# GpSimd makes the low part of a weight tile in four operations of 256 columns in place of one of 1024

## The chip, the cores and the metric

The kernel runs on one core of a Trainium2 chip. The metric is the device time of one launch in microseconds (us). Of the kernel before, three timed runs gave 2517.66, 2519.01 and 2524.25 us, so the median is 2519.01 us.

## The reference, cut to what matters

One layer of a decoder trunk on 256 tokens of width 2048, all in float32. The part that the change touches is the second sub-layer, a retrieval of experts by product keys (cut):

```python
def peer(h, w_q, sub_keys, w_up, w_down):
    qp = (h @ w_q).reshape(B, S, PEER_HEADS, 2, PEER_HALF)
    s = jnp.einsum('bshpe,hpne->bshpn', qp, sub_keys)
    v1, i1 = lax.top_k(s[..., 0, :], PEER_TOPK)
    v2, i2 = lax.top_k(s[..., 1, :], PEER_TOPK)
    cand = (v1[..., :, None] + v2[..., None, :]).reshape(B, S, PEER_HEADS, -1)
    top, ci = lax.top_k(cand, PEER_TOPK)
    idx = e1 * PEER_NKEYS + e2              # e1, e2: the two key numbers of ci
    g = jax.nn.softmax(top, axis=-1)
    # per token: 128 of 16384 experts, one row of w_up and one of w_down each
    a = gelu(einsum('td,tkd->tk', x, w_up[idx]))
    return einsum('tk,tkd->td', g * a, w_down[idx])
```

The first sub-layer (convolution, dilated attention, gates) comes before it and holds none of the changed operations.

## The kernel before

Every float32 product is made of three products of rounded parts: a weight tile is split into `hi`, the tile rounded, and `lo`, the tile less `hi`, and TensorE multiplies hi by hi, lo by hi and hi by lo. Weights stream from memory in units of 128x2048; a unit has two halves of 128x1024 columns, and a half is the step of the program. For each half ScalarE makes `hi` (`split_a`, L84), then VectorE or GpSimd makes `lo` (`split_b`, L88), then TensorE runs the products (`mm`). The class `Stream` writes the instructions of each engine in a fixed order: `hi` is written three halves and `lo` two halves ahead of the products, and background work of VectorE (`spread`) is put between. There are four buffers of `hi` and three of `lo`.

The retrieval does not gather: it multiplies with all 16384 experts and weighs with a gate matrix that is zero for those not chosen. The up products run over four quarters of 32 units (`up_unit`). There a unit must be transposed first: VectorE writes `wt` (L1250, two buffers), ScalarE and GpSimd read it. A half is 24 matmuls: for each of 8 blocks of 128 columns L1265 (hi), L1266 (hi again, other factor) and L1267, which uses 128 columns of `lo` as its weights.

Which engine makes `lo` is chosen by `pool_lo`. GpSimd makes it for all 64 halves of the first quarter and the first 36 of the second (100 in a row, with nothing else to do on GpSimd but one IOTA), for 16 halves of the last quarter, and for one half of two in the second pass of the down products of three quarters (`down_unit`, 48 halves). VectorE makes the others.

Beside the 100 halves VectorE has two background works: the top-16 search (L1134 to L1224, up to about 1160 us) and then, one step behind each half, the gate matrix (`gate_c`): five tensor_tensor operations, L1331, L1334 and three times L1338, whose results feed 24 small matmuls (L1347), which TensorE runs after that half's products, and L1354, which reads the product from PSUM.

Of the kernel before, what the change touches and what calls it, by code (L numbers as in the profile page):

```python
# [8 lines left out]
F32 = mybir.dt.float32  # L9
# [5 lines left out]
OP = mybir.AluOpType  # L15
# [51 lines left out]
def layer_kernel(ctx, tc, x, c, norm1_g, norm2_g, w_ada, b_ada, w_in, conv_dw, conv_db, conv_ln_g,  # L67
                 conv_ln_b, w_conv_out, b_conv_out, q_norm_g, k_norm_g, w_attn_o, w_out, peer_w_q,
                 peer_sub_keys, peer_w_up, peer_w_down, out):
    nc = tc.nc  # L70
# [14 lines left out]

    def split_b(h, src, eng):
        h.lo = main.tile([P, 1024], F32R, name="lo", tag="lo", bufs=LO_BUFS)
        eng.tensor_tensor(h.lo, src, h.hi.bitcast(F32), op=OP.subtract)  # L88

    turn = [0]  # L90

# [6 lines left out]
    def weight_unit(w_ap, mm, after=((), ()), pool_lo=(False, False)):  # L98

        u = Unit(None, [])  # L100

        def load():
            raw = load_raw()
            view = raw.rearrange("p (a b) -> p a b", a=4)
            if isinstance(w_ap, list):
                for i, ap in enumerate(w_ap):
                    part = view[32 * i:32 * (i + 1)] if ap.ap[0][1] == 32 else view[:, :, P * i:P * (i + 1)]
                    nc.sync.dma_start(part, ap)
            else:
                nc.sync.dma_start(view, w_ap)  # L110
            u.raw = raw

        u.load = load
        for n in range(2):
            h = Half(mm=lambda h, n=n: mm(n, h.hi.rearrange("p (a b) -> p a b", a=2),
                                          h.lo.rearrange("p (a b) -> p a b", a=2)),
                     after=after[n])
            h.a = lambda h, n=n: split_a(h, u.raw[:, n * 1024:(n + 1) * 1024])
            h.b = lambda h, n=n: split_b(h, u.raw[:, n * 1024:(n + 1) * 1024],
                                         nc.gpsimd if pool_lo[n] else nc.vector)  # L120
            h.unit = u
            u.halves.append(h)
        return u
# [421 lines left out]
    def start_half(u, n, blk, k, k0, k1):  # L545

        src = lambda: u.raw[:, n * 1024:(n + 1) * 1024]

        def mm(h):
            hi, lo = (w.rearrange("p (a b) -> p a b", a=2) for w in (h.hi, h.lo))  # L550
            if k == k0:
                blk.open(k0)
            for t in range(2):
                z = blk.ps[t]
                for kk in range(2):
                    first, last = blk.ends(k + kk, k0, k1)
                    nc.tensor.matmul(z, lhsT=h_hi(k + kk, t), rhs=hi[:, kk], start=first, stop=False)
                    nc.tensor.matmul(z, lhsT=h_hi(k + kk, t), rhs=lo[:, kk], start=False, stop=False)
                    nc.tensor.matmul(z, lhsT=h_lo(k + kk, t), rhs=hi[:, kk], start=False, stop=last)  # L559

        h = Half(mm=mm, a=lambda h: split_a(h, src()), b=lambda h: split_b(h, src(), nc.vector))
        if k == k1 - 2:
            h.after = [lambda: blk.close(k0, k1)]
        u.halves.append(h)
# [668 lines left out]
    def up_unit(q, r, pool_lo):  # L1233
# [11 lines left out]
        for n in range(2):  # L1245
            h = Half(mm=None, uses_raw_in="a")

            def a(h, n=n):
                wt = T2["pool"].tile([P, 8, 4, 32], F32, name="wt", tag="wt", bufs=2)
                nc.vector.transpose(wt.rearrange("p j g a -> p g j a"),  # L1250
                                    u.raw.rearrange("p (g j a) -> p g j a", g=4, a=32)[:, :, n * 8:(n + 1) * 8, :])
                cell[n] = wt.rearrange("p j g a -> p (j g a)")
                split_a(h, cell[n])

            def b(h, n=n):
                split_b(h, cell[n], nc.gpsimd if pool_lo(r, n) else nc.vector)

            def mm(h, n=n):
                if n == 0 and r % 2 == 0:
                    C["ps"] = T2["ps"].tile([P, 2, T], F32, name="aps", tag="qp", bufs=2)  # L1260
                z = C["ps"][:, r % 2, :]
                hi, lo = (v.rearrange("p (j e) -> p j e", j=8) for v in (h.hi, h.lo))
                for jj in range(8):
                    j = 8 * n + jj
                    nc.tensor.matmul(z, lhsT=hi[:, jj], rhs=qh["hi"][:, j, :], start=j == 0, stop=False)  # L1265
                    nc.tensor.matmul(z, lhsT=hi[:, jj], rhs=qh["lo"][:, j, :], start=False, stop=False)  # L1266
                    nc.tensor.matmul(z, lhsT=lo[:, jj], rhs=qh["hi"][:, j, :], start=False, stop=j == NK - 1)  # L1267

            h.a, h.b, h.mm = a, b, mm
            if n == 1 and r % 2 == 1:  # L1270
                h.after = [lambda: up_done(q, r - 1, C["ps"])]
            u.halves.append(h)
# [343 lines left out]
```

## Time and profile before

| what | value |
|---|---|
| median of three runs | 2519.01 us |
| profiled execution | 2518.21 us, its span 2516.4 us |
| TensorE busy | 2426.6 us (96%) |
| VectorE busy | 1854.2 us (74%) |
| ScalarE busy | 1120.8 us (45%) |
| GpSimd busy | 530.3 us (21%) |
| tensor_tensor of L88 on GpSimd | 116 with `wt` (mean 2529 ns), 48 with `raw` (mean 2436 ns) |
| granted TensorE clock | 0.989 of full speed, mean |

PE is TensorE's matmuls, PEld its weight loads, DVE VectorE, ACT ScalarE, POOL GpSimd. A matmul's row shows a modelled end, so a busy PE can hide short gaps: its pace is better read from the starts. In a timeline, rows are merged where one engine repeats a line; the bracket gives idle time before the row and what ended it.

### The profile page before, as it was taken

The page shows a single profiled execution, that of the slowest core. Times are in us where ns is not written, and L with a number is a line of the kernel's source. Part 1 is how long each engine was busy: PE and PEld are TensorE (multiplying, and loading weights), DVE is VectorE, ACT ScalarE, POOL GpSimd, SP SyncE. Part 2 cuts the span into 40 slices and gives each one's busy share as a digit, 9 for nine tenths or more (in the row PEclk, how much of TensorE's full clock was granted, in tenths as well). Part 3 has the DMA queues.
Part 4 walks back from the last instruction along what each step waited for, and adds up shares of the span by engine and source line. Part 5 has one row for each costly group of instructions (what it writes and reads, how often), then busy time and mean ns, then how long its engine had stood idle before and what let it go on. Part 6 is the DMA issues. An engine that isn't in the chain of part 4 may idle for free.

```text
span 2516.4 us, 39750 instructions
## 1 busy us (share of the span) xinstructions
PE 2426.6 (96%) x15728; PEld 2056.6 (82%) x15728; DVE 1854.2 (74%) x2642; ACT 1120.8 (45%) x1477; POOL 530.3 (21%) x262
## 2 busy tenths in 40 slices
PE   7999889999999899988999999999999999999998
PEld 4667677777766799988889988999987899988877
DVE  2655679886454569897998787877799777667776
ACT  5333345444334444443335555555443344445454
POOL 1000000000000007786552234332000111124023
PEclk9999999999999999999999999999999999999999
DMA  9887346777899978777557866899844777766563
GB/s 329 297 301 251 117 136 210 257 251 267 279 298 294 204 159 178 158 167 152 110 124 220 234 218 194 222 226 238 204 156 135 185 181 185 188 186 214 194 209 117
DMA packets 261178, 518.73 MB, mean 206 GB/s; under 512 B 16400, under 2 KB 57568, under 8 KB 260352
## 3 DMA queue, kind: packets, MB, share of 16 engines
q1 hardware_dynamic: 258912, 507.61, 70.4%
q0 software_dynamic: 2048, 8.58, 1.0%
q8 instruction: 123, 2.02, 0.4%
q14 instruction: 63, 0.52, 0.1%
q10 hardware_dynamic: 32, 0.01, 0.0%
HBM read 511.94 MB, written 4.19 MB: 205 GB/s over the span
## 4 chain that ended last, share of the span: by engine, by line
PE 71%; DVE 10%; POOL 3%; issue 2%; DMA 1%; ACT 1%; SPq 0%; DVEq 0%; POOLq 0%; ACTq 0%
PE aps L1267 6%; PE aps L1265 6%; PE aps L1266 6%; PE y L1435 6%; PE y L1436 6%; PE y L1438 5%; PE z L429 5%; PE z L431 4%; PE z L430 4%; PE z L1436 3%; PE z L1438 3%; PE z L1435 3%; POOL lo L88 3%; DVE wt L1250 2%; PE ada L330 2%
## 5 line engine op out<-in xcount | busy, mean ns | idle before, releaser
L88 DVE TENSOR_TENSOR lo<-raw,hi 128x1024 fp32r<-128x1024 f32 x456 | 561.8, 1237 | 376.3 <-issue 112.6
L84 ACT CAST hi<-raw 128x1024 fp32r<-128x1024 f32 x504 | 526.6, 1051 | 520.6 <-PE zv L559 103.1
L1267 PE MATMUL aps<-h2hi,lo 128*128 128x256 f32 x2048 | 582.0, 284 | 8.6 <-POOL lo L88 8.5
L1265 PE MATMUL aps<-h2hi,hi 128*128 128x256 f32 x2048 | 584.3, 285 | 0.4 <-ACT hi L84 0.4
L1266 PE MATMUL aps<-h2lo,hi 128*128 128x256 f32 x2048 | 580.7, 284 | 0.0
L84 ACT CAST hi<-wt 128x1024 fp32r<-128x1024 f32 x256 | 269.3, 1052 | 470.7 <-DVE wt L1250 427.6
L88 POOL TENSOR_TENSOR lo<-wt,hi 128x1024 fp32r<-128x1024 f32 x116 | 292.7, 2529 | 611.1 <-PE aps L1267 497.1
L1267 PEld LDWEIGHTS aps<-h2hi,lo 128*128 128x128 f32 x2048 | 394.0, 192 | 11.2 <-POOL lo L88 11.2
L1265 PEld LDWEIGHTS aps<-h2hi,hi 128*128 128x128 f32 x2048 | 394.1, 192 | 2.6 <-ACT hi L84 0.6
L1266 PEld LDWEIGHTS aps<-h2lo,hi 128*128 128x128 f32 x2048 | 394.3, 193 | 2.0 <-issue 0.2
L1250 DVE STREAM_TRANSPOSE wt<-raw 128x1024 f32<-128x1024 f32 x256 | 315.8, 1237 | 28.2 <-POOL lo L88 23.7
L1418 DVE TENSOR_TENSOR ccl<-C,cch 128x256 fp32r<-128x256 f32 x248 | 198.9, 803 | 96.7 <-PE z L1438 57.6
L1435 PE MATMUL y<-hi,cch 128*128 128x512 f32 x608 | 241.1, 397 | 0.0
L1436 PE MATMUL y<-lo,cch 128*128 128x512 f32 x608 | 237.3, 390 | 0.0
L88 DVE TENSOR_TENSOR lo<-wt,hi 128x1024 fp32r<-128x1024 f32 x140 | 171.8, 1229 | 27.3 <-PE aps L1267 14.0
L1438 PE MATMUL y<-hi,ccl 128*128 128x512 f32 x608 | 187.6, 390 | 0.0
L88 POOL TENSOR_TENSOR lo<-raw,hi 128x1024 fp32r<-128x1024 f32 x48 | 117.0, 2436 | 245.9 <-PE z L1436 123.6
L347 POOL TENSOR_TENSOR acc<-acc,raw 128x512 f32<-128x512 f32 x60 | 101.4, 1689 | 261.0 <-ACT raw L346 240.3
L1413 ACT CAST cch<-C 128x256 fp32r<-128x256 f32 x248 | 99.8, 403 | 123.6 <-PE z L1436 101.9
L1436 PE MATMUL z<-lo,cch 128*128 128x512 f32 x384 | 149.5, 389 | 2.2 <-DVE lo L88 2.2
L1435 PE MATMUL z<-hi,cch 128*128 128x512 f32 x384 | 149.5, 389 | 1.0 <-ACT cch L1413 1.0
L1438 PEld LDWEIGHTS y<-hi,ccl 128*128 128x128 f32 x608 | 114.2, 188 | 24.4
(295 smaller groups left out, 3965.7 us busy)
## 6 DMA issues: line engine op xcount, KB each, us to landing
raw<-in_peer_w_up_dram SPq DMA_DIRECT2D x512, 256.0 KB, 6.0
raw<-in_peer_w_down_dram SPq DMA_DIRECT2D x128, 1024.0 KB, 5.1
raw<-in_w_ada_dram SPq DMA_DIRECT2D x86, 1024.0 KB, 7.1
raw<-in_w_in_dram SPq DMA_DIRECT2D x73, 1024.0 KB, 5.3
raw<-in_w_out_dram SPq DMA_DIRECT2D x64, 256.0 KB, 5.2
raw<-in_peer_w_q_dram SPq DMA_DIRECT2D x64, 256.0 KB, 7.1
raw<-in_w_in_dram SPq DMA_DIRECT2D x22, 512.0 KB, 8.9
raw<-in_w_ada_dram SPq DMA_DIRECT2D x20, 512.0 KB, 5.2
```

Source lines behind the costliest of these rows:

```text
L84: nc.scalar.copy(h.hi, src)
L88: eng.tensor_tensor(h.lo, src, h.hi.bitcast(F32), op=OP.subtract)
L347: nc.gpsimd.tensor_tensor(acc, acc, src, op=OP.add)
L429: nc.tensor.matmul(z, lhsT=ah, rhs=hi[:, kk], start=first, stop=False)
L1250: nc.vector.transpose(wt.rearrange("p j g a -> p g j a"), u.raw.rearrange("p (g j a) -> p g j a", g=4, a=32)[:, :, n * 8:(n + 1) * 8, :])
L1265: nc.tensor.matmul(z, lhsT=hi[:, jj], rhs=qh["hi"][:, j, :], start=j == 0, stop=False)
L1266: nc.tensor.matmul(z, lhsT=hi[:, jj], rhs=qh["lo"][:, j, :], start=False, stop=False)
L1267: nc.tensor.matmul(z, lhsT=lo[:, jj], rhs=qh["hi"][:, j, :], start=False, stop=j == NK - 1)
L1418: nc.vector.tensor_tensor(cl, row, ch, op=OP.subtract)
L1435: nc.tensor.matmul(z, lhsT=ch, rhs=hi, start=first, stop=False)
L1436: nc.tensor.matmul(z, lhsT=ch, rhs=lo, start=False, stop=False)
L1438: nc.tensor.matmul(z, lhsT=cl, rhs=hi, start=False, stop=last)
```

## The change

`split_b` issues, where the engine is GpSimd, four subtractions of 256 columns on slices of the same three tiles. On VectorE it stays at one of 1024.

```diff
     def split_b(h, src, eng):
         h.lo = main.tile([P, 1024], F32R, name="lo", tag="lo", bufs=LO_BUFS)
-        eng.tensor_tensor(h.lo, src, h.hi.bitcast(F32), op=OP.subtract)
+
+        n = 256 if eng is nc.gpsimd else 1024
+        for i in range(0, 1024, n):
+            eng.tensor_tensor(h.lo[:, i:i + n], src[:, i:i + n], h.hi[:, i:i + n].bitcast(F32), op=OP.subtract)
```

On GpSimd, at the start of the up products, `lo<-wt,hi` stands for the operation of L88 and the bracket names the engines on whose counts it waits. Before:

```order
L1068 IOTA iota_rep 128x256
L88 TENSOR_TENSOR lo<-wt,hi 128x1024 [waits PE_49,Activation_49] x9
L1161 IOTA small_7763 128x256
L88 TENSOR_TENSOR lo<-wt,hi 128x1024 [waits PE_49,Activation_49] x91
L347 TENSOR_TENSOR acc<-acc,raw 128x512 [waits DMAHW5_49,Activation_49]
```

The same place with the change, where the line is L91 and the rows around the second IOTA are shown:

```order
L91 TENSOR_TENSOR lo<-wt,hi 128x256 [waits PE_49,Activation_49]
L91 TENSOR_TENSOR lo<-wt,hi 128x256 x3
L1164 IOTA small_7790 128x256
L91 TENSOR_TENSOR lo<-wt,hi 128x256 [waits PE_49,Activation_49]
L91 TENSOR_TENSOR lo<-wt,hi 128x256 x3
```

The first piece of a half waits for what the whole operation waited for, and the other three wait for nothing; the order of the halves is the same.

On TensorE, at the start of a half in the same stretch, before:

```order
L1265 MATMUL aps<-h2hi,hi 128x256 [waits Activation_49]
L1266 MATMUL aps<-h2lo,hi 128x256
L1267 MATMUL aps<-h2hi,lo 128x256 [waits Pool_49]
L1265 MATMUL aps<-h2hi,hi 128x256
L1266 MATMUL aps<-h2lo,hi 128x256
```

With the change, at the end of a half and the start of the next one (L1268 to L1270 are the same three lines):

```order
L1268 MATMUL aps<-h2hi,hi 128x256
L1269 MATMUL aps<-h2lo,hi 128x256
L1270 MATMUL aps<-h2hi,lo 128x256 [waits Pool_49]
L1268 MATMUL aps<-h2hi,hi 128x256
L1269 MATMUL aps<-h2lo,hi 128x256
L1270 MATMUL aps<-h2hi,lo 128x256
L1268 MATMUL aps<-h2hi,hi 128x256
L1269 MATMUL aps<-h2lo,hi 128x256
L1270 MATMUL aps<-h2hi,lo 128x256
L1268 MATMUL aps<-h2hi,hi 128x256 [waits Activation_49]
L1269 MATMUL aps<-h2lo,hi 128x256
L1270 MATMUL aps<-h2hi,lo 128x256 [waits Pool_49]
```

A half waited once for GpSimd, at its first matmul with `lo`; now it waits four times, at each sixth matmul, once for each piece. No instruction of VectorE, ScalarE, TensorE or of the DMA queues changes its place.

## Rows read from the trace of the kernel before

**Rows 1.** The page: span, busy time by engine, and the larger group of L88.

```profile
span 2516.4 us, 39750 instructions
PE 2426.6 (96%) x15728; PEld 2056.6 (82%) x15728; DVE 1854.2 (74%) x2642; ACT 1120.8 (45%) x1477; POOL 530.3 (21%) x262
...
L88 POOL TENSOR_TENSOR lo<-wt,hi 128x1024 fp32r<-128x1024 f32 x116 | 292.7, 2529 | 611.1 <-PE aps L1267 497.1
```

**Rows 2.** Windows: length, busy PE, PEld, DVE, ACT, POOL, clock, DMA share.

```profile
952.00:1160.00 208.00, 199.01 (x1629) 195.82 (x1628) 180.12 (x342) 87.70 (x99) 168.96 (x68) 1.00 0.80 171
...
1212.00:1316.00 104.00, 97.92 (x1154) 92.57 (x1153) 100.01 (x164) 35.20 (x57) 60.54 (x24) 1.00 0.53 122
...
1480.00:1610.00 130.00, 129.00 (x669) 110.73 (x668) 98.68 (x90) 70.33 (x99) 52.82 (x23) 1.00 0.67 198
```

**Rows 3.** Waits of TensorE, 952 to 1160 us: total, times, longest.

```profile
PE aps L1267 <- POOL lo L88: 8.5, 11, 1.9
```

**Rows 4.** Waits of TensorE, 1160 to 1316 us.

```profile
PE gps L1347 <- DVE ohg L1338: 11.9, 7, 4.2
```

**Rows 5.** Timeline of GpSimd in the up products: start, duration of the row, operation.

```profile
952.17 2.41 POOL L88 TENSOR_TENSOR lo<-wt,hi 128x1024 fp32r<-128x1024 f32 x1 [81.24 <-PE qp L1100]
...
1069.91 2.36 POOL L88 TENSOR_TENSOR lo<-wt,hi 128x1024 fp32r<-128x1024 f32 x1 [5.46 <-ACT hi L84]
...
1149.36 17.33 POOL L88 TENSOR_TENSOR lo<-wt,hi 128x1024 fp32r<-128x1024 f32 x7 [3.06 <-ACT hi L84]
```

**Rows 6.** Timeline of GpSimd: a tensor_tensor of 512 columns after an idle time.

```profile
1334.71 1.29 POOL L347 TENSOR_TENSOR acc<-acc,raw 128x512 f32<-128x512 f32 x1 [23.39 <-ACT raw L346]
```

**Rows 7.** Timeline of GpSimd: two memsets, one behind the other, at the start.

```profile
3.17 0.54 POOL L297 MEMSET silu_c<- 128x512 f32 x1
3.63 0.32 POOL L444 MEMSET uT<- 128x240 f32 x1
```

**Rows 8.** Timeline of VectorE: one operation blocked, the same one shortly after.

```profile
1021.38 3.05 DVE L1206 TENSOR_TENSOR C<-C,small 128x1024 bf16<-128x1024 bf16 x1
...
1029.87 1.23 DVE L1206 TENSOR_TENSOR C<-C,small 128x1024 bf16<-128x1024 bf16 x1
```

**Rows 9.** Timeline of VectorE beside the seven operations of GpSimd from 1149.36.

```profile
1162.79 1.70 DVE L1331 TENSOR_TENSOR oh<-iota_rep,e2T 128x1024 bf16<-128x1024 bf16 x1
1164.41 2.56 DVE L1334 TENSOR_TENSOR oh<-iota_rep,e1T 128x512 bf16<-128x512 bf16 x1
```

**Rows 10.** Timeline of VectorE: a gate step with GpSimd idle.

```profile
1184.37 1.23 DVE L1250 STREAM_TRANSPOSE wt<-raw 128x1024 f32<-128x1024 f32 x1
...
1185.84 0.67 DVE L1331 TENSOR_TENSOR oh<-iota_rep,e2T 128x1024 bf16<-128x1024 bf16 x1
1186.44 0.41 DVE L1334 TENSOR_TENSOR oh<-iota_rep,e1T 128x512 bf16<-128x512 bf16 x1
1186.88 1.09 DVE L1338 TENSOR_TENSOR ohg<-oh,gp 128x512 bf16<-128x512 bf16 x3
1187.89 1.24 DVE L1250 STREAM_TRANSPOSE wt<-raw 128x1024 f32<-128x1024 f32 x1
```

**Rows 11.** Timeline of GpSimd in the gate steps.

```profile
1174.20 2.62 POOL L88 TENSOR_TENSOR lo<-wt,hi 128x1024 fp32r<-128x1024 f32 x1 [7.51 <-PE aps L1267]
...
1214.69 2.40 POOL L88 TENSOR_TENSOR lo<-wt,hi 128x1024 fp32r<-128x1024 f32 x1 [1.28 <-PE aps L1267]
...
1244.50 2.58 POOL L88 TENSOR_TENSOR lo<-wt,hi 128x1024 fp32r<-128x1024 f32 x1 [1.71 <-PE aps L1267]
...
1308.75 2.58 POOL L88 TENSOR_TENSOR lo<-wt,hi 128x1024 fp32r<-128x1024 f32 x1 [1.71 <-PE aps L1267]
```

**Rows 12.** Timeline of VectorE: a gate step with GpSimd at work.

```profile
1240.45 1.24 DVE L1250 STREAM_TRANSPOSE wt<-raw 128x1024 f32<-128x1024 f32 x1
...
1241.92 1.42 DVE L1331 TENSOR_TENSOR oh<-iota_rep,e2T 128x1024 bf16<-128x1024 bf16 x1
...
1244.73 1.24 DVE L1250 STREAM_TRANSPOSE wt<-raw 128x1024 f32<-128x1024 f32 x1
```

## The prediction

> **What bounds the kernel now.** I read the page first, then windows by stage, then what TensorE waited for in each stage, then the timelines of GpSimd and VectorE where it waited. On the page TensorE is busy 96% of the span, VectorE 74%, GpSimd 21% [rows 1], which says that GpSimd matters only locally. The windows show where. From 1480 to 1610 us, the second down pass of the first quarter, TensorE is busy for 129.00 of 130 us [rows 2]: what GpSimd does there costs nothing as long as it is on time. The two stages in which GpSimd makes every low part are different. From 952 to 1160 us TensorE lacks 9.0 us of 208, and 8.5 us of that are 11 waits for GpSimd's `lo` [rows 2, 3]; GpSimd is busy for 168.96 us there. From 1212 to 1316 us VectorE is busy for 100.01 of 104 us and TensorE for 97.92 [rows 2]: the gate steps are bound by VectorE, and between 1160 and 1316 us TensorE waits 11.9 us for its L1338 [rows 4]. So the change is worth what it does in about 364 us, in two stages with different limits.
>
> **The price of four pieces.** The trace has no subtraction of 256 columns. An operation that starts after an idle time takes 2.41 us for 1024 columns [rows 5] and 1.29 us for 512 [rows 6]: 1.12 us for 512 columns more, so 0.17 us are fixed, and a piece is 0.17 + 0.56 = 0.73 us. Four after each other would be 2.92 us. But durations overlap where nothing is waited for: a memset of 0.54 us is followed by the next 0.46 us after its start [rows 7], 0.08 less. Only the first piece of a half waits, so three pieces may gain up to 0.08 each: 2.68. I take 2.80 us a half, the middle. The ends: 2.41 us if the fixed part overlaps entirely, and, if a small operation costs twice the fixed part that these two rows show, 4 x 0.90 = 3.60 us.
>
> [...]
>
> **Stage one, 952 to 1160 us.** 68 operations took 168.96 us [rows 2], or 2.48 each: 2.41 and 0.07 in which VectorE held the port. With 2.80 they take 68 x 2.87 = 195 us of 208. GpSimd is still not the bound, but its share goes from 81% to 94%, so it can no longer catch up: seven in a row took 17.33 us [rows 5], 2.48 each, and would take 20.1. The end from which it decides is (208 - 5) / 68 = 2.99 us a half.
>
> Against this stand two gains. First, TensorE waited for the whole of `lo`; now it waits for its first quarter, ready after 0.73 instead of 2.41 us, and uses the pieces at 6 matmuls each. None of the 11 waits was longer than 1.9 us [rows 3], and 1.68 us come off each, so nearly all of the 8.5 us would go if GpSimd started each half when it does now. Second, a VectorE operation with two operands in SBUF stands still while GpSimd works: L1206 took 3.05 us in one place and 1.23 in another [rows 8]. After the change it waits for a piece, not for a whole operation, so the search is done sooner and the next transpose too. Idle times of GpSimd of 5.46 and 3.06 us [rows 5], where the search waits for TensorE, absorb a lag that has grown up. Of the 8.5 us gained I count 3, since GpSimd starts later in the long runs. Ends: -8.5 us, all waits gone; and at 3.60 us a half, 68 x 3.67 = 250 us, +42 us.
>
> **Stage two, the gate steps.** How the two engines share the port is seen at 1162 us. GpSimd has seven operations ready from 1149.36 to 1166.69 [rows 5]. L1331 takes 1.70 us, where it takes 0.67 with GpSimd idle; L1334, right behind, takes 2.56 instead of 0.41 [rows 9, 10]. So after one VectorE operation GpSimd's next one came first, and after it VectorE's: where both are ready they alternate, operation by operation, whatever the length.
>
> A step free of this takes 1187.89 - 1184.37 = 3.52 us [rows 10]. From 1214.69 to 1308.75 us there are 23 operations of GpSimd, 22 steps of 4.28 us [rows 11]; the 0.76 us are L1331 waiting (1.42 against 0.67 [rows 10, 12]). From 1174.20 to 1214.69 us nine operations make 8 steps of 5.06 us [rows 11], with two VectorE operations blocked in turn.
>
> Now the steps with pieces that hold the port 0.53 us after 0.17 us of start. From the start of the transpose (0 us) the first operation that needs the port comes at 1.47 us [rows 12]; then L1331 holds it 0.60, L1334 0.44, three L1338 0.34 each [rows 10]. GpSimd starts 4.05 us after the transpose (1244.50 less 1240.45 [rows 11, 12]), when TensorE has finished a half. With GpSimd starting at 0: pieces one and two end at 0.70 and 1.40, L1331 runs from 1.47 to 2.07, piece three to 2.60, L1334 to 3.04, piece four to 3.57, two L1338 to 4.25, then the first piece of the next half, started at 4.05, goes before the third L1338: 5.12 us. The next step has three pieces left; they end at 0.53, 1.23, 1.93; L1331 waits 0.46 us; the step ends at 3.98, and the following one begins as the first did. The mean is 4.55 us. So the later 22 steps lose 22 x 0.27 = 6 us and the earlier 8 gain 8 x 0.51 = 4 us: +2 us. Ends: if only the piece under way blocks, 3.98 us a step, -6.6 and -8.6, together -15 us; if all four pieces block each step, 5.64 us, +30 and +5, together +35 us.
>
> **The rest.** The 48 halves of the down passes and 16 of the last quarter lie where TensorE is busy throughout, as from 1480 to 1610 us, where GpSimd works for 52.82 of 130 us [rows 2]: 0.39 us more a half is hidden by that idle time. If it were gone, all 64 would cost 25 us; no row speaks for that. TensorE's added waits are taken as 0: that stage has such waits too, and TensorE idles for 1.00 us in it.
>
> **The sum.** 2518.21 - 3 + 2 = 2517 us against the profiled execution, which is 0.8 us under the median; I say 2517, no change. What a measurement of this kernel can tell from no change is 0.3%, 7.6 us.
>
> **Rivals.**
> *VectorE goes through (faster).* If VectorE's next operation asks for the port before GpSimd's next piece does, a row of five tensor_tensors runs undisturbed and only the remainder of one piece blocks. For it: a piece needs 0.17 us to start, and VectorE's queue is full. Against it: L1334 lost to a waiting operation [rows 9]. With stage one at -8: 2518 - 15 - 8 = 2495 us.
> *GpSimd becomes the bound (slower).* Place: 952 to 1160 us. Price: at 3.36 us a half (fixed part 0.32 instead of 0.17) 68 x 3.43 = 233 us, 25 over the 208, less some 5 that a lead of two halves absorbs: +20; the gate steps, with more of GpSimd's time in each, +6. 2544 us. It decides from 2.99 us a half, 0.19 above what I take, and a fixed part of 0.2 without overlap gives that. For it: transposes wait for `wt` too. Against it: the durations of two sizes [rows 5, 6].
> *Pieces run into each other (slower).* If the port is not let go between pieces that wait for nothing, VectorE is blocked for 2.8 us where it was for 2.41, and the gate steps stay at or above 5 us: 22 x 0.8 = +18, the search as now: 2536 us. No row has GpSimd operations with two operands and without waits between them.
> A sentence of the Trainium skill speaks for that (GPSIMD Engine Reference, section 2.1, on dispatch): a core begins the next instruction when its own share of the last one is done, with no barrier. No row here shows it for this operation.
>
> **How the numbers follow.** Forecast 0.46 (own range 2507 to 2528), VectorE through 0.27 (2488 to 2508), GpSimd the bound 0.16, pieces together 0.11. Faster by over 0.3% is below 2511.4: most of the second and a seventh of the first, 0.31. Slower is above 2526.6: the last two and a part of the first, 0.29. Same: 0.40. The range leaves out a part of each end: 2493 to 2541.
>
> **What would show it.** Right: pieces of 0.70 to 0.75 us from start to start; TensorE waits for `lo` under 4 us up to 1160; L1331 or L1334 blocked by about 0.5 us and never by 2; gate steps of unequal length with a mean of 4.4 to 4.7 us. Wrong: GpSimd without idle time from 952 to 1160 and TensorE's waits for `lo` above 10 us (the bound), steps near 3.6 to 4.0 us (VectorE through), or single blocks of over 1 us (pieces together).

## The result and the profile after

The changed kernel takes 2533.14 us (median of 4 runs, 2531.34 to 2534.85) against 2518.34 us (4 runs, 2517.28 to 2524.25): a ratio of 1.0054 with a 95% interval of 1.0036 to 1.0071, 14.8 us slower. The forecast was 2517 us, no change. The measured change is about twice the 7.6 us that the prediction took as the least that can be told from none; the time lies inside the stated range, which the rivals had made wide.

The changed kernel has three lines more, so L88 is now L91, L1250 is L1253, L1331 is L1334, and so on; in the experiments below the shift is a different one. The page of the kernel after, its span, busy time by engine and the larger group of GpSimd's pieces answer to [rows 1]; the last row is an operation of VectorE in the down products:

```profile
span 2533.1 us, 40335 instructions
PE 2435.9 (96%) x15728; PEld 2061.2 (81%) x15728; DVE 1787.5 (71%) x2642; ACT 1120.3 (44%) x1477; POOL 621.2 (25%) x754
...
L91 POOL TENSOR_TENSOR lo<-wt,hi 128x256 fp32r<-128x256 f32 x464 | 352.0, 795 | 565.7 <-PE aps L1270 467.7
...
L1421 DVE TENSOR_TENSOR ccl<-C,cch 128x256 fp32r<-128x256 f32 x248 | 128.0, 518 | 95.0 <-PE z L1441 55.9
```

The same operation of VectorE on the page before:

```profile
L1418 DVE TENSOR_TENSOR ccl<-C,cch 128x256 fp32r<-128x256 f32 x248 | 198.9, 803 | 96.7 <-PE z L1438 57.6
```

VectorE is busy for 67 us less than before, since it is blocked for shorter times: this one line, with as many operations, takes 71 us less. GpSimd is busy for 91 us more. The shares do not tell whose time counts. The windows of the kernel after, with the columns of [rows 2], do so in part:

```profile
1480.00:1610.00 130.00, 128.38 (x655) 109.53 (x655) 77.99 (x90) 71.20 (x100) 65.27 (x72) 1.00 0.64 195
952.00:1160.00 208.00, 195.63 (x1568) 191.18 (x1566) 173.06 (x344) 83.19 (x95) 187.35 (x251) 0.98 0.76 163
1212.00:1316.00 104.00, 90.10 (x1087) 84.09 (x1087) 103.24 (x160) 31.64 (x50) 74.06 (x92) 1.00 0.52 120
```

From 1480 to 1610 us VectorE gained 20 us and TensorE was busy as before (128.38 against 129.00 us): the gain is worth nothing there. From 952 to 1160 us TensorE issued 1568 matmuls where it issued 1629: it fell behind by some 61 matmuls while GpSimd was busy for 187 of 208 us. The waits of TensorE in the kernel after, from 952 to 1190 us (total, times, longest), answer to [rows 3, 4]:

```profile
PE gps L1350 <- DVE ohg L1341: 7.1, 1, 7.1
PE aps L1270 <- POOL lo L91: 6.0, 10, 0.7
PE aps L1268 <- ACT hi L84: 6.0, 3, 3.9
```

Single waits for `lo` are shorter (0.7 against 1.9 us), but a wait for `hi` of 3.9 us is new (before, one of 0.4 us was all) and the first gate step is waited for 7.1 us where it was 4.2. All waits up to the first gate step come to 19.3 us, where they were 13.1.

`hi` comes late because `wt` does. VectorE can write the next `wt` only when GpSimd has read an earlier one, as there are two buffers. These waits of VectorE, before (952 to 1174 us) and after (952 to 1190 us), have grown by 11 us:

```profile
DVE wt L1250 <- POOL lo L88: 23.7, 22, 2.5
DVE wt L1253 <- POOL lo L91: 34.6, 28, 2.9
```

Where the time was lost is read from the timeline of GpSimd, since it works through the 100 halves in one fixed order. Before, with the rows that [rows 5, 11] leave out:

```profile
1020.94 8.28 POOL L88 TENSOR_TENSOR lo<-wt,hi 128x1024 fp32r<-128x1024 f32 x3 [3.21 <-ACT hi L84]
1029.96 5.91 POOL L88 TENSOR_TENSOR lo<-wt,hi 128x1024 fp32r<-128x1024 f32 x2 [0.75 <-ACT hi L84]
...
1052.24 12.22 POOL L88 TENSOR_TENSOR lo<-wt,hi 128x1024 fp32r<-128x1024 f32 x5 [0.78 <-ACT hi L84]
```

After, the same stretches (four pieces are a half). The search runs twice, for 128 tokens each time. At the end of each, TensorE transposes its results, ScalarE copies them and VectorE runs a chain of small operations; this is called the hand-over here, near 1070 and 1155 us:

```profile
953.00 8.56 POOL L91 TENSOR_TENSOR lo<-wt,hi 128x256 fp32r<-128x256 f32 x12 [81.01 <-PE qp L1103]
...
1018.22 2.83 POOL L91 TENSOR_TENSOR lo<-wt,hi 128x256 fp32r<-128x256 f32 x4 [0.26 <-ACT hi L84]
1023.59 47.30 POOL L91 TENSOR_TENSOR lo<-wt,hi 128x256 fp32r<-128x256 f32 x60 [2.55 <-ACT hi L84]
1076.40 5.57 POOL L91 TENSOR_TENSOR lo<-wt,hi 128x256 fp32r<-128x256 f32 x8 [5.50 <-ACT hi L84]
...
1111.69 44.49 POOL L91 TENSOR_TENSOR lo<-wt,hi 128x256 fp32r<-128x256 f32 x56 [3.24 <-ACT hi L84]
1159.29 19.41 POOL L91 TENSOR_TENSOR lo<-wt,hi 128x256 fp32r<-128x256 f32 x28 [3.11 <-ACT hi L84]
1186.38 3.38 POOL L91 TENSOR_TENSOR lo<-wt,hi 128x256 fp32r<-128x256 f32 x4 [7.68 <-PE aps L1270]
```

| stretch of GpSimd's work | before, us | after, us | loss |
|---|---|---|---|
| first 22 halves: 952.17 to 1020.94; 953.00 to 1023.59 | 68.8 | 70.6 | 1.8 |
| 15 halves to the hand-over of the first search: to 1069.91; to 1076.40 | 49.0 | 52.8 | 3.8 |
| to the seven halves of the second hand-over: to 1149.36; to 1159.29 | 79.5 | 82.9 | 3.4 |
| to the first half of the gate steps: to 1174.20; to 1186.38 | 24.8 | 27.1 | 2.3 |
| the search stage in whole | 222.0 | 233.4 | 11.4 |
| 30 gate steps, to 1308.75; to 1322.55 | 134.6 | 136.2 | 1.6 |

The finding is the rows with many pieces and no idle time inside: 15 halves in 47.30 us and 14 in 44.49, 3.15 and 3.18 us a half. Before, GpSimd had idle times of 0.75 us after each two or three halves there. So GpSimd has become the bound in these stretches. Grouped by line, the 15 halves before (count, then busy us, mean ns, idle time, of which 3.21 us lie ahead of the first half, and its releaser):

```profile
L88 POOL TENSOR_TENSOR lo<-wt,hi 128x1024 fp32r<-128x1024 f32 x15 | 39.9, 2674 | 6.8 <-ACT hi L84 6.2
```

They ran from 1020.94 to 1064.46 us, 2.90 us a half, of which 2.66 were busy: 2.41 of GpSimd's own and 0.25 that are put down to VectorE holding the port. GpSimd was idle for 0.24 us a half, and the change asks for 0.42 more (a half in four pieces takes 2.83 us where nothing blocks it, as at 1018.22). 15 x (3.15 - 2.90) = 3.8 us, which is the loss of that stretch.

At the hand-over the loss turns into other names. At the first one the search's transposes on TensorE start at 1063.37 us (before 1060.38), VectorE's chain of small operations behind them holds back the next `wt` to 1073.95 (before 1067.52), and TensorE has no lead left. TensorE's timeline after:

```profile
1076.38 0.58 PE L1268 MATMUL aps<-h2hi,hi 128*128 128x256 f32 x1 [3.90 <-ACT hi L84]
```

The clock then granted to TensorE (windows: length, busy PE, clock, DMA share, GB/s), with the second hand-over in the last row:

```profile
1072.00:1076.00 4.00, 0.48 (x5) 0.92 0.00 0
1076.00:1080.00 4.00, 3.61 (x15) 0.50 0.89 197
1080.00:1084.00 4.00, 4.00 (x27) 0.73 0.71 156
1160.00:1164.00 4.00, 3.93 (x20) 0.59 0.91 197
```

Two windows of the kernel before, with the same columns:

```profile
1076.00:1080.00 4.00, 3.98 (x33) 1.00 0.99 215
1160.00:1164.00 4.00, 3.35 (x28) 1.00 0.98 205
```

After 3.9 us of idle time the clock is at its lower level, 1.2 GHz; before, the longest wait at this place was 1.9 us [rows 3], and the clock stayed at the upper one. 4 x 0.50 + 4 x 0.27 = 3.1 us of work at full speed are lost by it, an estimate from these rows; they are part of the 3.4 us of the third line of the table, not more. At the second hand-over TensorE waits 1.5 us for `hi` and 0.3 for `lo`, and the clock is at 0.59 in the window behind: 4 x 0.41 = 1.6 us more by the same estimate. The added waits of 6.2 us and the slower clock, 4.7 us, make 10.9 of the 11.4 us that the search stage lost.

The gate steps look much as the prediction's walk through two of them had it. VectorE after, one short and one long step, to set beside [rows 10, 12] (L1334, L1337 and L1341 are L1331, L1334 and L1338 there):

```profile
1259.30 1.23 DVE L1253 STREAM_TRANSPOSE wt<-raw 128x1024 f32<-128x1024 f32 x1
...
1260.77 1.15 DVE L1334 TENSOR_TENSOR oh<-iota_rep,e2T 128x1024 bf16<-128x1024 bf16 x1
1261.84 0.41 DVE L1337 TENSOR_TENSOR oh<-iota_rep,e1T 128x512 bf16<-128x512 bf16 x1
1262.29 1.09 DVE L1341 TENSOR_TENSOR ohg<-oh,gp 128x512 bf16<-128x512 bf16 x3
1263.30 1.24 DVE L1253 STREAM_TRANSPOSE wt<-raw 128x1024 f32<-128x1024 f32 x1
...
1264.77 1.27 DVE L1334 TENSOR_TENSOR oh<-iota_rep,e2T 128x1024 bf16<-128x1024 bf16 x1
1265.96 0.96 DVE L1337 TENSOR_TENSOR oh<-iota_rep,e1T 128x512 bf16<-128x512 bf16 x1
1266.95 1.62 DVE L1341 TENSOR_TENSOR ohg<-oh,gp 128x512 bf16<-128x512 bf16 x3
1268.50 1.23 DVE L1253 STREAM_TRANSPOSE wt<-raw 128x1024 f32<-128x1024 f32 x1
```

The steps are 4.00 and 5.20 us long in turn, 4.60 in the mean (walk: 3.98, 5.12 and 4.55). In the short one L1334 is blocked for 0.48 us; in the long one L1334, L1337 and one L1341 are, for 0.53 to 0.60 us each.

### The profile page after: what moved, and what is told of

It reads as the page before. It is cut to its first block, busy times and chain, and to the rows that moved or that the text cites. A ratio compares the mean times of both kernels' runs of the same rounds, so it can differ in the third digit from the quotient of the medians.

```text
span 2533.1 us, 40335 instructions
## 1 busy us (share of the span) xinstructions
PE 2435.9 (96%) x15728; PEld 2061.2 (81%) x15728; DVE 1787.5 (71%) x2642; ACT 1120.3 (44%) x1477; POOL 621.2 (25%) x754
## 5 line engine op out<-in xcount | busy, mean ns | idle before, releaser
L91 DVE TENSOR_TENSOR lo<-raw,hi 128x1024 fp32r<-128x1024 f32 x456 | 566.4, 1247 | 447.5 <-issue 113.1
L1268 PE MATMUL aps<-h2hi,hi 128*128 128x256 f32 x2048 | 585.5, 286 | 6.0 <-ACT hi L84 6.0
L1270 PE MATMUL aps<-h2hi,lo 128*128 128x256 f32 x2048 | 583.4, 285 | 6.2 <-POOL lo L91 6.0
L91 POOL TENSOR_TENSOR lo<-wt,hi 128x256 fp32r<-128x256 f32 x464 | 352.0, 795 | 565.7 <-PE aps L1270 467.7
L1270 PEld LDWEIGHTS aps<-h2hi,lo 128*128 128x128 f32 x2048 | 394.9, 193 | 9.9 <-POOL lo L91 9.8
L1268 PEld LDWEIGHTS aps<-h2hi,hi 128*128 128x128 f32 x2048 | 395.1, 193 | 8.6 <-ACT hi L84 6.6
L1253 DVE STREAM_TRANSPOSE wt<-raw 128x1024 f32<-128x1024 f32 x256 | 315.8, 1237 | 43.0 <-POOL lo L91 34.6
L91 POOL TENSOR_TENSOR lo<-raw,hi 128x256 fp32r<-128x256 f32 x192 | 148.5, 803 | 217.2 <-issue 100.4
L1421 DVE TENSOR_TENSOR ccl<-C,cch 128x256 fp32r<-128x256 f32 x248 | 128.0, 518 | 95.0 <-PE z L1441 55.9
L91 DVE TENSOR_TENSOR lo<-wt,hi 128x1024 fp32r<-128x1024 f32 x140 | 170.6, 1221 | 27.1 <-PE aps L1270 14.0
```

What stands on the lines that cost most here:

```text
L91: eng.tensor_tensor(h.lo[:, i:i + n], src[:, i:i + n], h.hi[:, i:i + n].bitcast(F32), op=OP.subtract)
L1253: nc.vector.transpose(wt.rearrange("p j g a -> p g j a"), u.raw.rearrange("p (g j a) -> p g j a", g=4, a=32)[:, :, n * 8:(n + 1) * 8, :])
L1421: nc.vector.tensor_tensor(cl, row, ch, op=OP.subtract)
```

## The experiments

Each starts from the kernel before; `split_b` takes a list of column ranges for GpSimd, one operation for each. WHOLE is one range of 1024, FOUR four of 256, q the quarter of the up products, r the unit in it. The search stage is q = 0 (64 halves), the gate steps q = 1 (36, of which the first five are made ahead of the gate steps and lie in the search span below). All were timed in rounds with the kernel before on the same chip. "Search" and "gate" below are the two spans of GpSimd's timeline as in the table above (222.0 and 134.6 us before).

| run | search | gate | both, less before | median, less before | ratio, 95% interval |
|---|---|---|---|---|---|
| after | 233.4 | 136.2 | +13.0 | +14.8 | 1.0036 to 1.0071 |
| e1_search | 230.7 | 130.6 | +4.7 | +5.6 | 1.0011 to 1.0038 |
| e2_gate | 223.7 | 136.2 | +3.4 | +3.7 | 1.0002 to 1.0022 |
| e3_late | 222.0 | 134.6 | -0.1 | 0.0 | 0.9986 to 1.0005 |
| e4_repeat | 236.3 | 134.6 | +14.3 | +10.0 | 1.0028 to 1.0065 |
| e5_short | 219.0 | 134.6 | -2.9 | -4.0 | 0.9973 to 0.9993 |
| e6_two | 223.6 | 142.1 | +9.1 | +9.3 | 1.0025 to 1.0049 |
| e7_less | 213.2 | 130.7 | -12.7 | -13.5 | 0.9933 to 0.9967 |
| e8_share | 242.4 | 134.5 | +20.4 | +20.9 | 1.0061 to 1.0102 |
| e9_sixth | 225.6 | 134.6 | +3.6 | +3.1 | 0.9999 to 1.0024 |
| e10_first | 226.7 | 132.6 | +2.7 | -1.2 | 0.9992 to 1.0011 |
| e11_second | 225.4 | 134.6 | +3.4 | +1.9 | 0.9995 to 1.0015 |

The sum of two spans in one profiled execution gives the timed difference within 2 us in ten of the twelve rows; e4 and e10 are some 4 us off (e4's profiled execution took 5.0 us more than its median; for e10 see below). So the cause of the change's cost lies in these 357 us.

**One stage at a time: e1_search, e2_gate, e3_late.**

```diff
-split_b(h, cell[n], nc.gpsimd if pool_lo(r, n) else nc.vector)
+split_b(h, cell[n], nc.gpsimd if pool_lo(r, n) else nc.vector, FOUR if q == 0 else WHOLE)   # e1
+split_b(h, cell[n], nc.gpsimd if pool_lo(r, n) else nc.vector, FOUR if q == 1 else WHOLE)   # e2
+split_b(h, cell[n], nc.gpsimd if pool_lo(r, n) else nc.vector, FOUR if q == 3 else WHOLE)   # e3, and FOUR in the down products
```

> Four pieces only for the 64 halves of the first quarter, where the search runs; whole operations everywhere else. Rate theory (GpSimd's 2.83 us a half in place of 2.41 costs in the search stage): most of the loss is here, +7 to +11 us, and TensorE again waits about 4 us for hi behind the search's hand-over near 1070 us. Gate theory (the loss is that short pieces block VectorE in the gate steps): 0 to +2 us. Wait theory (TensorE's three added waits a half cost time themselves): +5 us or so, spread evenly.

Measured 2525.64 us against 2520.01. The search stage alone costs 8.7 us up to the gate steps, and the wait for `hi` of 3.9 us is there, as the rate theory had it; that 4.0 us are given back in the gate steps was not expected and puts the time, +5.6 us, under its +7. GpSimd in e1, the first gate step and the steps from the fifth on, with whole operations:

```profile
1185.29 2.41 POOL L93 TENSOR_TENSOR lo<-wt,hi 128x1024 fp32r<-128x1024 f32 x1 [6.97 <-PE aps L1272]
...
1204.69 2.41 POOL L93 TENSOR_TENSOR lo<-wt,hi 128x1024 fp32r<-128x1024 f32 x1 [1.28 <-PE aps L1272]
1208.81 2.58 POOL L93 TENSOR_TENSOR lo<-wt,hi 128x1024 fp32r<-128x1024 f32 x1 [1.70 <-PE aps L1272]
1213.09 2.59 POOL L93 TENSOR_TENSOR lo<-wt,hi 128x1024 fp32r<-128x1024 f32 x1 [1.70 <-PE aps L1272]
```

The steps lock into 4.28 us at 1204.69, 19.4 us after the first; before, they did so at 1214.69, 40.5 us after it [rows 11].

> Four pieces only for the 36 halves of the second quarter, whole ones elsewhere. Rate theory: +3 to +6 us, of which 2 in the seven halves in a row ahead of the gate steps and 1 to 3 in the gate steps, whose length alternates between 4.0 and 5.2 us, mean 4.6. Gate theory: +10 us or more. Wait theory: +3 us.

Measured 2523.75 us, +3.7, of which 1.7 lie ahead of the gate steps and 1.6 in them. The gate steps alternate as in the kernel after: GpSimd starts at 1254.17, 1258.19 and 1263.38 us, steps of 4.02 and 5.19 us.

> Four pieces only in the last quarter's up products and in the down products (64 halves), whole ones in the search and the gate steps. Rate theory and gate theory: 0, since TensorE is busy throughout there. Wait theory: TensorE waits for pieces there too, +2 to +3 us.

Measured 2520.03 us, ratio 0.9995 (0.9986 to 1.0005): the 64 late halves cost nothing. e1 and e2 add up to 9.3 us and the change costs 14.8. The table shows most of the rest: in e1, with whole operations, the gate steps take 130.6 us, with pieces 136.2 in e2 and after alike, so the 4.0 us that e1 gets back are not to be had. Some 1.5 us stay open. It is not the late end of the search as such that shortens e1's gate steps: they take 134.6 and 134.5 us behind a later search in e4 and e8, and 130.7 behind an earlier one in e7. What decides between these times is not shown.

**Time or number of operations: e4_repeat, e5_short, e6_two, e7_less.** All but e6 change q = 0 alone; e5 and e7 leave out `lo` of the last 192 columns, and the matmuls of the last two blocks read columns that are there.

```diff
+REPEAT = (0, 1024), (896, 1024)                          # e4: more time, no early piece
+SHORT = (0, 208), (208, 416), (416, 624), (624, 832)     # e5: four pieces, time as before
+TWO = (0, 512), (512, 1024)                              # e6: everywhere
+LESS = (0, 832),                                         # e7: one operation, less time
```

> In the first quarter a half is one operation of 1024 columns and a second one that makes its last 128 columns again, so GpSimd needs about 2.8 us a half as with four pieces, with one long block of the port in place of four short ones; the rest as before. Rate theory: +6 to +11 us, as with four pieces in this stage, perhaps more since TensorE has no early first piece. Port theory (the loss in the search is that each short VectorE operation waits for a piece): 0 to +3 us.

Measured 2529.97 us, +10.0, as the rate theory had it. Taking longer is enough, without four waits and four pieces. Nor is memory the cause: VectorE waits 5.0 us for `raw` in the search stage of the kernel after against 1.3 before, but 1.1 in e4, which loses more. GpSimd in e4, the 15 halves (two operations each), 3.21 us a half:

```profile
1025.46 48.22 POOL L93 TENSOR_TENSOR lo<-wt,hi 128x1024 fp32r<-128x1024 f32 x30 [3.50 <-ACT hi L86]
```

> In the first quarter four pieces of 208 columns in place of 256, so GpSimd needs about 2.4 us a half, as before the change, though in four pieces; the low parts of the last 192 columns are left out (the matmuls of the last two blocks read the columns of the block before). The rest as before. Rate theory (GpSimd's time per half costs, not the pieces): -3 to +2 us, no wait of TensorE for hi near 1070 us above 1 us. Port theory (the number of short blocks costs): +5 to +9 us, as with four pieces of 256 in this stage.

Measured 2517.12 us against 2521.15, 4 us faster. Four pieces that take no longer than one whole are a small gain, and the idle times are back in GpSimd's rows of e5:

```profile
1023.34 8.31 POOL L93 TENSOR_TENSOR lo<-wt,hi 128x208 fp32r<-128x208 f32 x12 [2.54 <-ACT hi L86]
1032.42 5.91 POOL L93 TENSOR_TENSOR lo<-wt,hi 128x208 fp32r<-128x208 f32 x8 [0.77 <-ACT hi L86]
```

So the early first piece does what the prediction said of it: TensorE waits 2.0 us in whole for `lo` from 952 to 1160 us in e5, where it waited 8.5 [rows 3].

> Two operations of 512 columns everywhere on GpSimd, about 2.55 us a half. Rate theory: a third of the way in the search, +2 to +4 us, and gate steps of 4.3 to 4.4 us, +0 to +2; together +2 to +6. Port theory: about half of the change's loss, +7.

Measured 2530.48 us against 2521.15: the search stage is nearly as before (+1.6 us at 2.55 us a half), but the gate steps are the worst of all, which was not expected to this size: +9.3 us lie outside the rate theory's +2 to +6. GpSimd in e6, the first and the last row of the 15 halves, then gate steps:

```profile
1022.31 8.57 POOL L93 TENSOR_TENSOR lo<-wt,hi 128x512 fp32r<-128x512 f32 x6 [2.54 <-ACT hi L86]
...
1055.40 12.63 POOL L93 TENSOR_TENSOR lo<-wt,hi 128x512 fp32r<-128x512 f32 x10 [0.64 <-ACT hi L86]
...
1227.67 2.95 POOL L93 TENSOR_TENSOR lo<-wt,hi 128x512 fp32r<-128x512 f32 x2 [0.69 <-PE aps L1272]
1233.44 3.00 POOL L93 TENSOR_TENSOR lo<-wt,hi 128x512 fp32r<-128x512 f32 x2 [2.82 <-PE aps L1272]
1237.13 2.94 POOL L93 TENSOR_TENSOR lo<-wt,hi 128x512 fp32r<-128x512 f32 x2 [0.69 <-PE aps L1272]
1244.41 2.73 POOL L93 TENSOR_TENSOR lo<-wt,hi 128x512 fp32r<-128x512 f32 x2 [4.34 <-PE aps L1272]
```

The gate steps take 3.69, 5.77 and 7.28 us: two pieces of over 1 us each block two or more operations in a long step.

> In the first quarter one operation of 832 columns, about 2.0 us a half; the low parts of the last 192 columns are left out (the matmuls of the last two blocks read the columns of the block before). The rest as before. Rate theory, if GpSimd's time was already part of the bound before the change: -3 to -8 us, TensorE's waits for lo below half of the 8.5 us. If the bound was VectorE alone there: 0.

Measured 2507.67 us against 2521.15, -13.5 us, more than expected; 8.8 us are gained in the search stage and 3.9 in the gate steps, whose instructions are as before. TensorE is busy for 202.14 of 208 us from 952 to 1160. GpSimd in e7, the first and the last row of the 15 halves:

```profile
1021.83 4.93 POOL L93 TENSOR_TENSOR lo<-wt,hi 128x832 fp32r<-128x832 f32 x2 [3.21 <-ACT hi L86]
...
1060.52 1.99 POOL L93 TENSOR_TENSOR lo<-wt,hi 128x832 fp32r<-128x832 f32 x1 [0.54 <-ACT hi L86]
```

So GpSimd's time was already part of the bound before the change, although it was idle now and then. Over all runs each of the 15 halves takes longer the more GpSimd works on it: 2.71 us at 1.99 us of its own (e7), 2.90 at 2.41 (before), 2.91 at 2.42 (e5), 3.05 at 2.55 (e6), 3.15 at 2.83 (after) and 3.21 at 2.91 (e4). That fits a chain that goes round: GpSimd frees `wt`, VectorE writes the next one, ScalarE makes `hi` of it, GpSimd goes on. A third buffer of `wt` would test this; no run has one.

**Other hands for GpSimd's work: e8_share, e9_sixth.**

```diff
+SHARE = (0, 832),             # e8, q = 0, and behind it in split_b:
+if j < 1024:
+    nc.vector.tensor_tensor(h.lo[:, j:], src[:, j:], h.hi[:, j:].bitcast(F32), op=OP.subtract)
+fifth = lambda r, n: (2 * r + n) % 6 != 5    # e9, in place of `busy` in q = 0
```

> In the first quarter GpSimd makes 832 columns of a half's low part in one operation, about 2.0 us, and VectorE the other 192, about 0.3 us; the rest as before the change. Rate theory: GpSimd's 0.4 us a half come back as with 832 columns alone, less what VectorE's added 64 x 0.3 = 19 us cost, since VectorE is busy for about 87% of that stage: between -10 and +5 us, -3 as the middle. Port theory, where VectorE is the bound of the search: +10 us or more.

Measured 2540.58 us against 2519.7: missed. The window of e8 shows that VectorE has no room left: it is busy for 204.75 of 208 us.

```profile
952.00:1160.00 208.00, 184.37 (x1458) 177.79 (x1457) 204.75 (x391) 77.75 (x86) 120.91 (x60) 0.99 0.71 152
```

> In the first quarter VectorE makes the low part of every sixth half (10 of 64) in place of GpSimd, whole operations everywhere; the rest as before the change. Rate theory: GpSimd's share of the search falls by a sixth, VectorE gets 10 x 1.2 = 12 us: between -8 and +3 us. If VectorE is the bound of the search: +8 us or more.

Measured 2522.75 us against 2519.7, not told apart from no change and no gain. No version that computes all and beats the kernel before was found.

**Half of the search stage: e10_first, e11_second.** FOUR for q = 0 in the first 18 units alone (36 halves), or in the other 14 (28 halves).

```diff
+FOUR if q == 0 and r < 18 else WHOLE     # e10
+FOUR if q == 0 and r >= 18 else WHOLE    # e11
```

> Four pieces only in the first 36 halves of the first quarter, up to the first hand-over of the search near 1070 us; the rest as before the change. Rate theory with a lost lead: GpSimd and the transposes behind it reach the hand-over about 3 us late, TensorE waits 2 to 4 us for hi there at the end of its supply and then runs at the lower clock for some us: +3 to +6 us. If the loss grows evenly with the halves: 36/64 of the loss of all 64, +3.5 us, with no long wait.

Measured 2519.9 us against 2521.1 (ratio 0.9992 to 1.0011), no loss that can be told from none, where both theories had one. Its trace does show one: the hand-over comes late, TensorE waits 2.5 us for `hi` there, and the search stage takes 4.7 us longer; the gate steps then give 2.0 us back. GpSimd in e10 behind the hand-over:

```profile
1074.19 2.36 POOL L93 TENSOR_TENSOR lo<-wt,hi 128x1024 fp32r<-128x1024 f32 x1 [5.51 <-ACT hi L86]
```

> Four pieces only in the last 28 halves of the first quarter, behind the first hand-over; the rest as before the change. Rate theory with a lost lead: the same at the second hand-over, near 1155 us, and waits for lo in the stretch before it: +1 to +4 us, and no wait for hi above 1 us near 1070 us. Evenly: 28/64 of the loss, +2.5 us.

Measured 2523.03 us against 2521.1 (0.9995 to 1.0015). The median alone is not told apart from no change; in the trace the search stage takes 3.4 us longer, the gate steps as long as before. GpSimd in e11, 14 halves of the second search at 3.18 us:

```profile
1105.72 44.52 POOL L93 TENSOR_TENSOR lo<-wt,hi 128x256 fp32r<-128x256 f32 x56 [2.54 <-ACT hi L86]
```

In the search stage the halves add up: 4.7 + 3.4 = 8.1 us against e1's 8.7. So in the traces each search has its own loss, and nothing absorbs the first. That the median of e10 shows less than its trace comes from the execution that the trace is set against: e10's profiled execution took 2519.99 us, 1.8 more than the profiled one of the kernel before (2518.21), while the median before was 2521.1 in that round; and e10's search stage began 1.0 us earlier.

## Why the prediction was wrong

**The price of four pieces: right.** 2.80 us a half was taken and 2.83 measured, pieces 0.71 us apart where nothing blocks. (2.83 - 2.41) / 3 = 0.14 us is what the rows give for each added operation.

**Stage one: the step that failed.** "68 x 2.87 = 195 us of 208. GpSimd is still not the bound" counted -3 us for a stage that lost 11.4. It has three faults.

- It took room as a mean over the stage, with the port's share at 0.07 us a half. The x68 has the one IOTA in it; the 67 subtractions took 168.50 us, which makes the share 0.10. In the 15 halves beside L1206 it was 0.25 before and 3.15 - 2.83 = 0.32 after. There a half came every 2.90 us, and 2.90 - 0.32 leaves 2.58 us for GpSimd's own work, not 2.99.
- It took GpSimd's idle time for room. Even 2.58 is no sharp point: at 2.55 us (e6) GpSimd is still idle for 0.65 us now and then, and each of the 15 halves already takes 3.05 us.
- It priced only TensorE's wait for `lo`. That `wt` comes later when GpSimd frees it later stands among the rivals ("transposes wait for `wt` too") and in the sum at nothing; these waits of VectorE grew from 23.7 to 34.6 us, and behind them came the new waits for `hi`.

By GpSimd's own time a half the search stage gained 3.0 us at 2.42 (e5), lost 1.6 at 2.55 (e6), 8.7 at 2.83 (e1) and 14.3 at 2.91 without an early piece (e4). The mean of a stage hid two stretches with other operations beside them; their rows were in the trace before.

**The gain of 3 us: not had.** Shorter waits for `lo` came only where GpSimd was on time (e5). In the change the total fell from 8.5 to 6.0 us, and 5.6 us more of waits for `hi` and 2.9 more for the first gate step came in their place.

**The idle times that absorb a lag: wrong.** The 5.46 us before the hand-over were counted as room [rows 5]. They are not: after it, GpSimd still waits 5.50 us there, because that time belongs to the search's own chain, which begins later when GpSimd is late.

**Stage two: right, with a reservation.** Alternation operation by operation, steps of 3.98 and 5.12 us and +2 us were forecast; 4.00, 5.20 and +1.6 were measured. The terms were somewhat larger on both sides: the first 8 steps gained 5.5 us (forecast 4) and the later 22 lost 7.1 (forecast 6). In the long step the walk had the first of the five operations free and two of the last three blocked; it was the first, the second and one of the last three. The Trainium skill (SBUF — State Buffer, "Who interferes with whom") has the port as an exclusive lock for a whole operation; what stood still in the gate steps waited for 0.48 to 0.60 us, a piece at most, as that rule has it. What the walk took for granted is that before's steps always take 134.6 us; e1 shows that the same instructions can take 4 us less.

**The rest: right.** e3 bears out the 0. Of the 16.7 us by which the profiled spans differ, 13.8 are gone at the last of the 100 halves; the other 2.9 were not traced, and the four runs of the kernel after differ by 3.5.

**The rivals.** "GpSimd becomes the bound" (0.16) was the one that came, at the place it named and at about half of its price there (+11.4 us against +20), but with the point of decision too high and the cause in the port and in `wt`, not in the fixed part. Its price was also not its own: a fixed part of 0.32 us makes 3.40 us a half with the overlap taken above, not 3.36. "VectorE goes through" is excluded by the alternation, and "pieces run into each other" by the same rows: no operation of VectorE is blocked for more than 0.60 us there.

**The signs.** Three of the four signs of being right came (pieces 0.71 us apart, blocks of about 0.5 us, gate steps of 4.5 to 4.6 us in the mean). The fourth did not: TensorE waited 5.7 us for `lo` up to 1160, not under 4. But the sign of the bound, above 10 us of such waits, did not come either, since the loss stood under `wt`, `hi` and the clock.

## What to carry to other kernels

Cutting an operation into n pieces adds n - 1 fixed parts to its engine (0.14 us each here), and the consumer's earlier start pays for that only where the engine has room in each stretch. Look for room stretch by stretch, with what holds the engine up there, and not by its share of a stage: 81% busy was 0.24 us idle of 2.90 where it mattered. Ask of such idle time too whether it is room: here a half took longer whenever GpSimd did, and the next tile waited for the buffer that GpSimd was reading. An idle time in front of a dependent chain is no reserve, since a late producer moves the chain too.

## What the hardware showed that was not expected

- In the gate steps VectorE and GpSimd, with pieces 0.71 us apart, alternate and fall into a period of two steps (4.00 and 5.20 us). With pieces of 512 columns the steps are 3.69 to 7.28 us, 142.1 us for 30 against 134.6 with whole operations and 136.2 with quarters: an intermediate size was the worst.
- Steps with whole operations fall into a fixed phase of 4.28 us, but the time until they do differs between kernels that have the same instructions there: 30 steps took 130.6 (e1), 132.6 (e10) or 134.6 us (before).
- Behind a wait of 3.9 us TensorE's granted clock stood at 0.50 over the next 4 us and at 0.73 over the 4 after them; behind waits of 1.5 and 0.3 us at the second hand-over it stood at 0.59 over 4 us. Before, behind waits of 0.4 and 1.9 us at the first one, it stayed at 1.00.
